# One unread product ahead of every chunk of 24 weight products in the feed-forward up stages

## The chip, the cores and the metric

One core of a Trainium2 chip runs the whole network in one launch. The metric is the device time of a launch in microseconds (us); lower is better.

## What is computed

256 tokens of 1024 features, float32, go through two blocks of two layers each. The feed-forward layers, whose up stages the change touches, are these (cut from the reference):

```python
def conv_ffn(x, w_up, conv_w, conv_b, w_down):            # D_FF = 2816
    h = x @ w_up                                          # 1024 -> 5632
    h = lax.conv_general_dilated(h, ...) + conv_b         # 3 taps along the tokens
    gate, up = jnp.split(h, 2, axis=-1)
    return (jax.nn.silu(gate) * up) @ w_down

def swiglu(n, w_gate, w_up, w_down):
    return (jax.nn.silu(n @ w_gate) * (n @ w_up)) @ w_down
```

The first block has two layers, each a mixer (a gated recurrence, then a sparse attention) followed by `conv_ffn`. The second block has two layers of `swiglu`, a mixer (a spatial gating, then an attention over shared keys and values) and `swiglu` again; so there are four `swiglu` layers. Every layer's input is normed by the token's root mean square. Between the third `swiglu` layer's input and the second attention stand the shared keys, computed from the same tokens.

## The kernel before, in words

**Products.** Every weight product is done in two parts: weights and inputs are each split into a float32r part `hi` and a rest `lo`, and `hi*hi + hi*lo + lo*hi` is summed in PSUM. `unit` (L229) fetches 256 columns of a matrix for 1024 rows (1 MB, issued on SyncE's queue), writes `whi` on ScalarE (L249) and `wlo` on VectorE (L251). There are three buffers for fetched weights and four for each split part. `feat` (L255) does one chunk: for 8 blocks of 128 rows the three products L263, L264 and L265, each with 128x128 weights as the loaded operand and 256 tokens as the moving one: 24 products. `feat2` (L267) does the two chunks of a unit into the halves of one PSUM bank. `down` (L545) and `tok` (L280) do the same with the tokens loaded and 256 weight columns moving (L565 to L567, L576 to L578, L289 to L291).

**Up stages.** `conv_ffn` (L663) takes 11 steps `i`; each step has two units, gate and up, each followed by VectorE's and ScalarE's work on the result. `swiglu` (L626) takes 11 steps too, with L655 and L658 scaling the two results by the token factors. In the second, third and fourth `swiglu` layer (`p.halves`) the first step has a form of its own: it goes by token with `tok_turn` (L613), one tile of 128 tokens after the other; ScalarE's L645 and VectorE's L646 make `ffu` for each tile, and four transposes (L650) turn it into features. Behind its two tiles the program writes `p.finish()`, which broadcasts the token factors on TensorE (L370, copied to `rb` by ScalarE at L446) and, in the third `swiglu` layer, turns the input of the shared keys as well (`pre_half`, L407, transposes L412, splits L306 and L308). In that layer the shared keys themselves (`shared_kv`, L1497, with column sums L365, L1506, L1516 and the rotation product L1489) are written ahead of step 3. The first `swiglu` layer follows `block1_end` (L1315): the end of the first block norms the sum and forms one token factor from two (L1337 to L1341), and the broadcast L370 is the last TensorE work that the program writes ahead of the layer's first step. Here the first step has the common form.

**Order.** The program is written in one order; a compiler pass with a model of time then decides the order on every engine, taking an instruction that is ready ahead of one that is not, the earlier written one first. Where the program wants an order on TensorE, it ties what follows to the last TensorE instruction that it has written so far:

```python
    def behind(s):
        pe = mybir.EngineType.PE
        return s.tc.issue_after(next(i for i in reversed(s.nc.cur_bb.bb.instructions) if i.engine == pe))
```

Before the change the common `feat2` of the up stages has no such tie. PSUM has eight banks: four for `acc`, two for `mx` (transposes), two for `pr` (small products, broadcasts).

**The third mixer's bias rows.** Behind the first `conv_ffn` the program writes a table of 3 MB to DRAM (L1056); the sparse attention reads it back, and the queue of SyncE holds weights of that attention behind the reading.

Of the kernel before, what the change touches and what calls it, by code (L numbers as in the profile page):

```python
# [15 lines left out]
P = 128  # L16
D = 1024
T = 256
# [17 lines left out]
# buffers by tag: a tag's tiles are handed out in the order of the program  # L36
# [9 lines left out]
# a step's later parts, in steps behind its first, and the steps before which the queries' products come  # L46
# [7 lines left out]
# V values, N turned latent of the queries, P their rope part, R its rope, Q queries, S scores, T turned, O out  # L54
# [67 lines left out]
class Feat:  # L122
    """1024 or more features by 256 tokens, two chunks of 128 features to a tile"""
# [14 lines left out]
class Split:  # L138
    """a Feat in two parts, hi and lo, whose sum it is"""
# [8 lines left out]
class Net:  # L148
    def __init__(s, tc, ctx, a):
        s.tc, s.nc, s.a = tc, tc.nc, a  # L150
        s.posted = False
# [7 lines left out]
    # ---- tiles  # L159
# [32 lines left out]
    def behind(s):  # L192
        """what follows on TensorE is queued behind the last of its instructions so far"""
        pe = mybir.EngineType.PE
        return s.tc.issue_after(next(i for i in reversed(s.nc.cur_bb.bb.instructions) if i.engine == pe))

    def warm(s, n):
        """n products that nobody reads, behind the last of TensorE's instructions so far: its clock halves at rest"""
        if n:
            with s.behind():  # L200
                ps = s.prod()
                x = s.ident.bitcast(BF16)
                for _ in range(n):
                    s.nc.tensor.matmul(ps[:, :T], x[:, :P], x, start=True, stop=True)

    # ---- weights
    def fetch(s, parts, k0, nk, cuts=1):
        """columns of matrices, side by side, for k of 128 rows: on their way"""
# [14 lines left out]
    def begin(s, p, fine=0):  # L223
        """a layer: the first of its weights are split in smaller pieces"""
# [3 lines left out]
    def unit(s, parts, k0, nk, fetched=None):  # L228
        """the same, split in two"""  # L229
# [13 lines left out]
        with ExitStack() as stack:  # L243
            # behind what the layer waits for
# [10 lines left out]
    def feat(s, w, c, x, ps):  # L255
        """ps[c-th 128 columns of w, tokens] = w^T x over the unit's k."""
# [10 lines left out]
    def feat2(s, w, x, c=0, beside=None):  # L267
        """two chunks of columns in one bank; beside() after each, in this order on TensorE"""
        ps = s.acc()
        s.parts(lambda j: s.feat(w, c + j, x, ps[:, j * T:(j + 1) * T]), beside)  # L270
# [9 lines left out]
    def tok(s, w, cols, t, x, ps, ks=None):  # L280
        """ps[tokens of tile t, cols of w] = x^T w over the unit's k."""
# [11 lines left out]
    def tok2(s, w, x, beside=None):  # L293
        """both tiles of tokens by the 256 columns of a unit, in one bank"""
# [8 lines left out]
    def split_scaled(s, parts):  # L303
        """(hi, lo, source, scale) of several chunks: a tile's parts are all written before they are read"""
# [6 lines left out]
    # ---- norms  # L311
    class Sum:
        """squares summed over chunks; the last chunk is left apart"""

    def sumsq(s, sm, src, k, n, scale=None):
# [3 lines left out]
        if k == n - 4:  # L319
            # the table of the square root, ahead of its use  # L320
# [8 lines left out]
    def rsqrt(s, out, ss, n, eps, factor=1.0):  # L329
        """out = factor * (ss / n + eps) ** -0.5 on small tiles."""  # L330
# [14 lines left out]
    def rsqrt_v(s, out, ss, n, eps):  # L345
        """the same on VectorE alone: a first guess from the bits, then Newton's steps"""
# [13 lines left out]
    def colsum(s, sm, st):  # L360
        """per-token sums of feature-major tiles -> [128 tokens, 2] in a bank"""
# [5 lines left out]
    def bcast(s, r, st):  # L367
        """[128 tokens, 2] -> [128, 256] of a bank, the same on all partitions"""
# [12 lines left out]
    class Pre:  # L381
        """the input of a layer, normed and split: x(k). The token's factor is left to its consumer:
        r by token, rb along the free axis"""
# [8 lines left out]
    def pre_group(s, p, n, sums=True, bank=None):  # L392
        """256 features of h, turned and split, and their squares' sums"""
# [13 lines left out]
    def pre_half(s, p, t, m, sums=True):  # L407
        """the same for a half of the features of a tile of tokens"""
# [15 lines left out]
    def squares(s, ss, src, n):  # L424
        """the sums of squares by token of a group of 256 features, src by token tile"""
# [3 lines left out]
        if n == 2:  # L429
            # the table of the square root, ahead of its use  # L430
# [20 lines left out]
    # ---- start  # L451
    def load_vectors(s, g, parts, queue):
        """rows of 128 values -> one column of s.vectors each"""
# [81 lines left out]
    def conv_vectors(s, l):  # L535
        """the taps and biases of a layer's convolution"""
# [7 lines left out]
    # ---- feed-forward layers  # L544
    def down(s, w, hid, kn, out, n_beside=0):  # L545
        """out(n, ps) for the 4 groups of 256 columns of hid @ w, hid of kn chunks; ps by token tile"""
# [4 lines left out]
        for n in range(4 - out.late):  # L551
            both = n < n_beside
            if both:
                # the two tiles in one bank, zeroed for both: a chunk of hid serves both at once
# [25 lines left out]
        # the last units: a tile of tokens to its end, then the other  # L580
# [32 lines left out]
    def tok_turn(s, p, units, t, ps, at=()):  # L613
        """both units side by side for a tile of tokens, what p has left to do before the k's in at"""
# [11 lines left out]
    def swiglu(s, p, wg, wu, wd, out, beside=None):  # L626
# [3 lines left out]
        for i in range(KF // 2):  # L630
# [4 lines left out]
            if p.halves and i == 0:  # L635
                # by token: the first tile of tokens is there before the second
# [17 lines left out]
            ps = s.feat2(s.unit([(wg, i * T, T)], 0, KD), p.x)  # L654
            nc.vector.tensor_tensor(h2(g), h2(ps), s.rb2(p), op=OP.mult)  # L655
            nc.scalar.activation(g, g, AF.Silu)
            ps = s.feat2(s.unit([(wu, i * T, T)], 0, KD), p.x)
# [5 lines left out]
    def conv_ffn(s, p, l, out):  # L663
# [12 lines left out]
        for i in range(KF // 2):  # L676
            if l == 0 and i in (3, 6):
                # those of the next one
# [7 lines left out]
            for y, first in zip(ys, (0, KF)):  # L686
                c = first + 2 * i
                ps = s.feat2(s.unit([(w, c * P, T)], 0, KD), p.x)
# [25 lines left out]
    # ---- first block, layer 0  # L714
    def hgrn(s, p, first):
# [40 lines left out]
        def decay(pr):  # L756
            """the logarithms, summed from the start of a chunk"""
# [11 lines left out]
            # exp(x - bk) = k exp(x - b)  # L769
# [4 lines left out]
        def query(pr):  # L774
            """without the tokens' factor"""
# [5 lines left out]
        def offsets():  # L781
            """what lies between a chunk of 32 and the border of the two tiles of 128 tokens"""
# [990 lines left out]
```

## Time and profile before

| | |
|---|---|
| median of 2 runs | 1663.08 us (1660.65 and 1665.51) |
| profiled execution | span 1657.0 us, first to last instruction; its own time beside the span is not listed |
| TensorE busy | 1619.9 us, 98% of the span |
| VectorE busy | 1150.6 us, 69% |
| ScalarE busy | 913.8 us, 55% |
| mean granted TensorE clock | 0.994 |

The timed runs are whole launches and so longer than the span of the profile. In the profile PE is TensorE's products, PEld its weight loads, DVE VectorE, ACT ScalarE. Products overlap in the pipeline, and each is shown with 0.28 us though the next one starts long before its end; so prices are read from start to start. A plain f32 product shows as two records, a float32r or bf16 product and a transpose as one.

### The profile page before, as it was taken

How to read it: one execution, taken by the hardware profiler on the slowest of the kernel's cores; microseconds unless marked ns; L12 is line 12 of the kernel's file. 1: busy time of each engine (PE TensorE's matmuls, PEld its weight loads, DVE VectorE, ACT ScalarE, POOL GpSimd, SP SyncE). 2: the span in 40 equal slices, each digit the busy share in tenths (PEclk: the TensorE clock that was granted, in tenths of full speed). 3: DMA queues.
4: the chain of work that ended last, by engine and by line, in shares of the span. 5: the costliest groups of instructions: out<-in, count | busy, mean ns of one | idle time of the engine just before them, and what ended most of it. 6: DMA issues, size and time to landing. Idle time of an engine off the chain costs nothing.

```text
span 1657.0 us, 34152 instructions
## 1 busy us (share of the span) xinstructions
PE 1619.9 (98%) x14500; PEld 1606.8 (97%) x14502; DVE 1150.6 (69%) x1900; ACT 913.8 (55%) x1443; POOL 6.7 (0%) x28
## 2 busy tenths in 40 slices
PE   8989999995999999999999999999999999999998
PEld 7989999995999999999999999999999999999998
DVE  6986899654859886766667857664686647677653
ACT  7865766453656656544465546444564446665442
POOL 0000000000000000000000000000000000000000
PEclk9999999997999999999999999999999999999999
DMA  8731755678446566566847565556376565447562
GB/s 266 217 100 53 228 188 187 191 154 190 136 136 218 174 202 192 184 192 193 250 144 228 178 191 172 185 171 203 124 241 188 195 201 142 154 133 227 184 202 71
DMA packets 303821, 297.58 MB, mean 180 GB/s; under 512 B 14295, under 2 KB 300214, under 8 KB 303670
## 3 DMA queue, kind: packets, MB, share of 16 engines
q1 hardware_dynamic: 303622, 295.40, 57.8%
q8 instruction: 114, 1.87, 0.5%
q14 instruction: 37, 0.30, 0.1%
q10 hardware_dynamic: 48, 0.01, 0.0%
HBM read 291.19 MB, written 4.19 MB: 178 GB/s over the span
## 4 chain that ended last, share of the span: by engine, by line
PE 91%; DVE 3%; DMA 3%; ACT 2%; issue 1%; SPq 0%; DVEq 0%; ACTq 0%
PE acc L265 16%; PE acc L263 16%; PE acc L264 16%; PE acc L565 8%; PE acc L567 7%; PE acc L566 7%; PE acc L289 3%; PE acc L290 3%; PE acc L291 3%; DMA bias_rows<-rrow 2%; PE acc L576 2%; PE acc L578 2%; PE acc L577 1%; DVE wlo L251 1%; ACT whi L249 1%; PE pr L844 1%
## 5 line engine op out<-in xcount | busy, mean ns | idle before, releaser
L249 ACT ACTIVATE whi<-wst 128x2048 fp32r<-128x2048 f32 (+4 forms) x404 | 524.2, 1331 | 507.1 <-issue 225.3
L251 DVE TENSOR_TENSOR wlo<-wst,whi 128x2048 fp32r<-128x2048 f32 (+4 forms) x404 | 620.9, 1560 | 247.4 <-ACT whi L249 245.6
L263 PE MATMUL acc<-xh,whi 128*128 128x256 f32 x2416 | 671.9, 279 | 1.3 <-ACT xh L306 0.9
L264 PE MATMUL acc<-xl,whi 128*128 128x256 f32 x2416 | 671.8, 279 | 1.0 <-DVE xl L308 1.0
L265 PE MATMUL acc<-xh,wlo 128*128 128x256 f32 x2416 | 671.3, 279 | 0.5 <-DVE wlo L251 0.5
L264 PEld LDWEIGHTS acc<-xl,whi 128*128 128x128 f32 x2416 | 456.1, 189 | 1.7 <-DVE xl L308 1.4
L263 PEld LDWEIGHTS acc<-xh,whi 128*128 128x128 f32 x2416 | 453.4, 188 | 2.0 <-ACT xh L306 1.1
L265 PEld LDWEIGHTS acc<-xh,wlo 128*128 128x128 f32 x2416 | 454.2, 188 | 0.9 <-DVE wlo L251 0.7
L567 PE MATMUL acc<-wlo,fh 128*128 128x256 f32 x880 | 245.0, 279 | 0.0
L566 PE MATMUL acc<-whi,fl 128*128 128x256 f32 x880 | 244.1, 278 | 0.0
L565 PE MATMUL acc<-whi,fh 128*128 128x256 f32 x880 | 244.0, 278 | 0.0
L567 PEld LDWEIGHTS acc<-wlo,fh 128*128 128x128 f32 x880 | 165.2, 188 | 0.0
L566 PEld LDWEIGHTS acc<-whi,fl 128*128 128x128 f32 x880 | 165.1, 188 | 0.0
L565 PEld LDWEIGHTS acc<-whi,fh 128*128 128x128 f32 x880 | 164.9, 188 | 0.0
L289 PE MATMUL acc<-whi,xh 128*128 128x256 f32 x384 | 108.9, 283 | 0.0
L290 PE MATMUL acc<-whi,xl 128*128 128x256 f32 x384 | 107.0, 279 | 0.0
L291 PE MATMUL acc<-wlo,xh 128*128 128x256 f32 x384 | 107.0, 279 | 0.0
L289 PEld LDWEIGHTS acc<-whi,xh 128*128 128x128 f32 x384 | 72.1, 188 | 0.2
L290 PEld LDWEIGHTS acc<-whi,xl 128*128 128x128 f32 x384 | 72.1, 188 | 0.0
L291 PEld LDWEIGHTS acc<-wlo,xh 128*128 128x128 f32 x384 | 72.1, 188 | 0.0
L658 DVE TENSOR_TENSOR ffu<-acc,rb 128x512 f32<-128x512 f32 x41 | 28.3, 690 | 46.5 <-PE acc L265 46.4
L308 DVE SCALAR_TENSOR_TENSOR xl<-mx,vectors,xh 128x128 fp32r<-128x128 f32 (+1 forms) x124 | 39.1, 375 | 22.9 <-ACT xh L306 22.8
(422 smaller groups left out, 2116.6 us busy)
## 6 DMA issues: line engine op xcount, KB each, us to landing
wst<-in_ffn_w_up_dram SPq DMA_DIRECT2D x88, 1024.0 KB, 5.3
wst<-in_ffn_w_down_dram SPq DMA_DIRECT2D x48, 1024.0 KB, 5.4
wst<-in_ffn_w_gate_dram SPq DMA_DIRECT2D x44, 1024.0 KB, 5.4
wst<-in_ffn_w_down_dram SPq DMA_DIRECT2D x24, 768.0 KB, 4.8
wst<-in_gmlp_w_in_dram SPq DMA_DIRECT2D x16, 1024.0 KB, 5.6
wst<-in_hgrn_w_in_dram SPq DMA_DIRECT2D x13, 1024.0 KB, 5.7
wst<-in_gmlp_w_out_dram SPq DMA_DIRECT2D x8, 1024.0 KB
wst<-in_dsa_w_in_dram SPq DMA_DIRECT2D x6, 1024.0 KB
```

What stands on the lines that cost most here:

```text
L249: s.nc.scalar.activation(hi[:, c], w[:, c], AF.Copy)
L251: s.nc.vector.tensor_tensor(lo[:, c], w[:, c], hi[:, c].bitcast(F32), op=OP.subtract)
L263: mm(ps, wh[:, k, cols], xh, start=k == 0, stop=False)
L264: mm(ps, wh[:, k, cols], xl, start=False, stop=False)
L265: mm(ps, wl[:, k, cols], xh, start=False, stop=k == nk - 1)
L289: mm(ps, xh[:, ts], wk, start=k == 0, stop=False)
L290: mm(ps, xl[:, ts], wk, start=False, stop=False)
L291: mm(ps, xh[:, ts], lk, start=False, stop=k == nk - 1)
L308: b = s.nc.vector.scalar_tensor_tensor(lo, src, g, hi.bitcast(F32), op0=OP.mult, op1=OP.subtract)
L565: mm(ps[t], xh, wh[:, k], start=k0 + k == 0 and not both, stop=False)
L566: mm(ps[t], xl, wh[:, k], start=False, stop=False)
L567: mm(ps[t], xh, wl[:, k], start=False, stop=k0 + k == kn - 1 and (t == 1 or not both))
```

## The change

`Net.between` (new) puts one product into a `pr` bank that nobody reads, tied behind the last TensorE instruction written; its kind goes round seven: none; bf16 with 64 columns; bf16 with 32 loaded and 32 moving columns; float32r with 16, 64 and 192 columns; bf16 with 128. All but the third load 128 columns. `feat2` gets an argument with which it calls `between` ahead of each of its two chunks and ties the chunk behind it. The calls in both up stages ask for it, `conv_ffn` from its second step on, `swiglu` in all steps of the common form. Comments are taken out elsewhere, which is not shown.

```diff
-        s.posted = False
+        s.posted, s.shape = False, 0
...
+    def between(s, x):
+
+        n, s.shape = s.shape, (s.shape + 1) % 7
+        mm = s.nc.tensor.matmul
+        with s.behind():
+            if n == 0:
+                return
+            ps = s.prod()
+            xh = x(0)[0]
+            if n == 1:
+                mm(ps[:, :64], s.identb, s.identb[:, :64], start=True, stop=True)
+            elif n == 2:
+                mm(ps[:32, :32], s.identb[:, :32], s.identb[:, :32], start=True, stop=True)
+            elif n == 3:
+                mm(ps[:, :16], xh[:, :P], xh[:, :16], start=True, stop=True)
+            elif n == 4:
+                mm(ps[:, :64], xh[:, :P], xh[:, :64], start=True, stop=True)
+            elif n == 5:
+                mm(ps[:, :192], xh[:, :P], xh[:, :192], start=True, stop=True)
+            else:
+                mm(ps[:, :P], s.identb, s.identb, start=True, stop=True)
+
+    def feat2(s, w, x, c=0, beside=None, between=False):
+
         ps = s.acc()
+        if between:
+            for j in range(2):
+                s.between(x)
+                with s.behind():
+                    s.feat(w, c + j, x, ps[:, j * T:(j + 1) * T])
+            return ps
         s.parts(lambda j: s.feat(w, c + j, x, ps[:, j * T:(j + 1) * T]), beside)
         return ps
...
-            ps = s.feat2(s.unit([(wg, i * T, T)], 0, KD), p.x)
+            ps = s.feat2(s.unit([(wg, i * T, T)], 0, KD), p.x, between=True)
...
-            ps = s.feat2(s.unit([(wu, i * T, T)], 0, KD), p.x)
+            ps = s.feat2(s.unit([(wu, i * T, T)], 0, KD), p.x, between=True)
...
-                ps = s.feat2(s.unit([(w, c * P, T)], 0, KD), p.x)
+                ps = s.feat2(s.unit([(w, c * P, T)], 0, KD), p.x, between=i > 0)
```

## Rows read from the trace of the kernel before

**Rows 1.** The page: span, busy time by engine, and the chain by engine.

```profile
PE 1619.9 (98%) x14500; PEld 1606.8 (97%) x14502; DVE 1150.6 (69%) x1900; ACT 913.8 (55%) x1443; POOL 6.7 (0%) x28
...
PE 91%; DVE 3%; DMA 3%; ACT 2%; issue 1%; SPq 0%; DVEq 0%; ACTq 0%
```

**Rows 2.** Timeline of TensorE, 250 to 256 us: start, duration, what.

```profile
249.73 0.28 PE L265 MATMUL acc<-xh,wlo 128*128 128x256 f32 x1
...
255.96 0.28 PE L263 MATMUL acc<-xh,whi 128*128 128x256 f32 x1
```

**Rows 3.** The page's groups: VectorE's scaling of the gated layers' up products.

```profile
L658 DVE TENSOR_TENSOR ffu<-acc,rb 128x512 f32<-128x512 f32 x41 | 28.3, 690 | 46.5 <-PE acc L265 46.4
```

**Rows 4.** Timeline of TensorE, 1233 to 1235 us.

```profile
1233.31 0.28 PE L365 MATMUL pr<-col,sqa 128*128 128x1 f32 x2
...
1234.44 0.28 PE L263 MATMUL acc<-xh,whi 128*128 128x256 f32 x1
```

**Rows 5.** The chain in order of time: start, duration, what.

```profile
90.45 1.48 PE pr L844 x64
```

**Rows 6.** Timeline of TensorE, 447 to 449 and 1416 to 1418 us.

```profile
448.36 0.39 PE L556 MATMUL acc<-cst,zero 128*128 128x512 bf16 x1
...
448.71 0.28 PE L566 MATMUL acc<-whi,zl 128*128 128x256 f32 x1
...
1416.35 1.03 PE L1489 MATMUL mx<-qrx,cst 128*128 128x256 f32 x4
1417.22 0.27 PE L1629 MATMUL acc<-maskb,identb 128*128 128x256 bf16 x1
```

**Rows 7.** Timelines of TensorE and VectorE, 665 to 679 us, first gated layer.

```profile
666.09 0.28 PE L263 MATMUL acc<-xh,whi 128*128 128x256 f32 x1
...
677.84 0.61 PE L370 MATMUL pr<-cst,f 128*128 128x128 f32 x4
678.21 0.37 PE L263 MATMUL acc<-xh,whi 128*128 128x256 f32 x1
...
674.66 0.16 DVE L1341 TENSOR_TENSOR f<-f,rc 128x2 f32<-128x2 f32 x1
```

**Rows 8.** Timelines of TensorE and VectorE, second and fourth gated layer.

```profile
1010.25 0.37 PE L263 MATMUL acc<-xh,whi 128*128 128x256 f32 x1
...
1018.28 0.38 PE L650 MATMUL mx<-cst,ffu 128*128 128x128 f32 x2
...
1016.49 0.48 DVE L646 SCALAR_TENSOR_TENSOR ffu<-acc,pr,ffg 128x256 f32<-128x256 f32 x1
...
1480.67 0.36 PE L263 MATMUL acc<-xh,whi 128*128 128x256 f32 x1
...
1486.64 0.48 DVE L646 SCALAR_TENSOR_TENSOR ffu<-acc,pr,ffg 128x256 f32<-128x256 f32 x1
```

**Rows 9.** Timelines of TensorE and VectorE, third gated layer, second step.

```profile
1199.83 0.37 PE L263 MATMUL acc<-xh,whi 128*128 128x256 f32 x1
...
1210.64 0.60 PE L650 MATMUL mx<-cst,ffu 128*128 128x128 f32 x4
...
1206.56 2.15 DVE L308 SCALAR_TENSOR_TENSOR xl<-mx,vectors,xh 128x128 fp32r<-128x128 f32 x8
```

**Rows 10.** Timelines of VectorE and TensorE, shared keys; in brackets idle time before it.

```profile
1228.97 0.69 DVE L1506 TENSOR_TENSOR kc<-acc,rb 128x512 f32<-128x512 f32 x1 [0.66 <-PE acc L265]
...
1233.07 0.42 DVE L1516 TENSOR_TENSOR krx<-acc,rb 128x256 f32<-128x256 f32 x1
...
1235.82 0.59 PE L1489 MATMUL mx<-krx,cst 128*128 128x256 f32 x2
```

**Rows 11.** Windows: stretch, its us, busy us of PE, PEld, DVE, ACT, POOL, granted clock, DMA.

```profile
380.00:382.00 2.00, 0.00 (x0) 0.00 (x0) 0.00 (x0) 0.00 (x0) 0.00 (x0) 0.53 0.88 101
395.00:397.00 2.00, 2.00 (x11) 2.00 (x11) 1.82 (x5) 0.00 (x0) 0.00 (x0) 0.50 1.08 346
```

**Rows 12.** Who waited for whom on TensorE: us in total, times, longest.

```profile
PE pr L1106 <- ACT drl L1109: 17.0, 2, 16.0
```

More of the change, by code (lines that the diff above doesn't have):

```diff
@@ L265, in feat @@
             mm(ps, wl[:, k, cols], xh, start=False, stop=k == nk - 1)
-    def feat2(s, w, x, c=0, beside=None):
-        ps = s.acc()
+    def between(s, x):
[19 more added lines that the diff above has]
+    def feat2(s, w, x, c=0, beside=None, between=False):
+        ps = s.acc()
+        if between:
[4 more added lines that the diff above has]
+            return ps
         s.parts(lambda j: s.feat(w, c + j, x, ps[:, j * T:(j + 1) * T]), beside)
@@ L312 @@
     class Sum:
+        pass
     def sumsq(s, sm, src, k, n, scale=None):
@@ L381 @@
     class Pre:
+        pass
     def pre(s, gain):
```

## The prediction

> **What bounds the kernel now.** I read the page's busy table and its chain first. TensorE is busy for 98% of the span and holds 91% of the chain that ended last [rows 1]. So whatever takes TensorE's time, or makes it stand, goes to the end nearly in full; what VectorE or ScalarE gain or lose counts only where TensorE waits for them. Next comes the price of a product. In an up stage the timeline has one start after the other: 56 products of 256 columns start between 249.73 and 255.96 us, which is 6.23 / 55 = 0.113 us each [rows 2]. A chunk of 24 is 2.72 us. Last I read the few places where TensorE's order in the trace differs from the order in which the program writes its products, because the change ties that order down [rows 7 to 10].
>
> **The change, part one: the products.** The two layers with a convolution call the new form in 10 of 11 steps, twice a step, two chunks a call: 80 chunks. The four gated layers call it in every step that runs the L655/L658 path; L658 ran 41 times [rows 3], so 41 x 2 x 2 = 164 chunks. Of 244 chunks every seventh, from the first on, gets nothing (35), so 209 products are added: 35 of each kind from one to five and 34 of the sixth.
>
> What a narrow product costs beside weight products is to be read where one already stands between them. In the shared-key part eight records with one moving column and 128x128 weights (L365) and two weight products start between 1233.31 and 1234.44 us: ten in 1.13 us, 0.113 us each [rows 4]. One column costs as much as 256. The stream goes at the pace of the weight loads, and each new product brings one, whatever it moves. A bf16 product of 512 columns between weight products (L556) shifts what follows: from its start to that of L566 there is 0.35 us, which holds it and one weight product, so 0.35 - 0.113 = 0.24 us [rows 6]. That is its columns, with hardly anything for the change of type. So I take 0.113 us for the five kinds of up to 128 columns: 174 x 0.113 = 19.7 us.
>
> The kind with 192 float32r columns is the open one, for the trace has no float32r product under 256 columns. If it goes as those of 256 do, it is 0.113 us. Plain f32 goes slower: four records of 256 columns (L1489, two per product) take 1416.35 to 1417.22, 0.2175 us each [rows 6]; by that pace 192 columns are 0.163 us a record, 0.33 us with two. I take one record at that pace, 0.16 us, between the two: 35 x 0.16 = 5.6 us. Part one is 25.3 us. The ends: if a narrow product needs no load period of its own it might cost as little as the 32-column products of L844, 64 in 1.48 us or 0.023 us [rows 5], 4.8 us for all 209; if float32r under 256 columns is always two plain records, the 70 of the third and fourth kind gain 0.113 us each and the 35 of the fifth 0.166 us, and the part is 39 us. The row with 128-column loads (L365) is the nearest, so I stay with 25.3. Nothing hides it: all of it stands on the engine that sets the end.
>
> The Trainium skill has a rule that would make it cheaper: "TensorE: Matmul & The Clock Gate", section "Back-to-back issue gap", gives isolated gaps of about 60 cycles for up to 64 columns and 134 for 128. By it, as an estimate from that page, 140 x 0.025 + 35 x 0.083 + 34 x 0.056 = 8.3 us. The row of L365 disagrees with it (0.113 us for one column), and the same section says that the isolated gap counts too little where every product has its own load.
>
> **Part two: the order.** Each new product, and each chunk behind it, is queued behind the last TensorE instruction that the program has written so far. Inside a stage this changes nothing, since chunks run in program order already. It does where the program writes, ahead of a chunk, TensorE work that has to wait, and where the compiler until now pulled chunks in front of it. There are five such places.
>
> (a) Start of the first gated layer of the second block. Its first step has the new form too, and the last TensorE work written ahead of it is the broadcast of the token factors (L370). Before, the step's 96 products start at 666.09 and the broadcast comes behind them, at 677.84 [rows 7]. The factor is ready when L341's chain ends with L1341, 674.66 + 0.16 = 674.82. Now the products wait for that and four records: 675.35. With 96 x 0.118 = 11.3 us (their pace from 666.09 to 677.84, four transposes among them) they end at 686.65 where before all was past at 678.21: 8.4 us.
>
> (b, c) Second step of the second and of the fourth gated layer. The first step goes by token, and its hidden part is turned (L650) behind VectorE's L646. Before, the second step starts at 1010.25 and the second pair of turns comes at 1018.28, in its midst [rows 8]. L646 ends at 1016.49 + 0.48 = 1016.97, late because weight splits are queued ahead of it on ScalarE and VectorE; these wait for no product of the second step, so the delay stays. The turns can start at about 1017.1 and the step at 1017.3: 7.0 us later, less 0.22 us for the pair that moved, 6.8. In the fourth layer it is 1486.64 + 0.48, and 0.3 more, 1487.4 for 1480.67 [rows 8]: 6.6 us.
>
> (d) Second step of the third gated layer. The same turns stand behind the transposes for the shared keys, whose two banks are freed by VectorE's L308; eight of these end at 1206.56 + 2.15 = 1208.71. The step can start at 1209.3 where it started at 1199.83 [rows 9]. Of the 9.5 us, 12 records (1.4 us) are work that moved ahead of it: 8.1 us.
>
> (e) Fourth step of that layer, behind the rotation of the shared keys (L1489). VectorE's L1506 shows the last chunk ahead done at 1228.9, the next ends 2.7 us later, at 1231.6, and L1489 waits for L1516 until 1233.49 [rows 10]; start at 1233.95, less 1.3 us for L365 and L1489, which fill the gap: 1.0 us.
>
> Together 30.9 us. In (a) to (d) TensorE rests for some 6 us and more. After its long rest in the third mixer the granted clock, which is 1.00 (2.4 GHz) in work, was 0.53 in 380 to 382, and back at work it was still 0.50 (1.2 GHz) in 395 to 397, with 11 records in these 2 us, where the full clock runs 17 [rows 11]. About 1.5 us of products are lost at such a return; 4 x 1.5 = 6.0 us (ends: none, and 8 if the slow stretch lasts longer). The ends of part two are 20 us (splits ordered anew, so that L646 comes some us sooner) and 45 us (the compiler, with TensorE standing, fills ScalarE and VectorE with still more splits ahead of what it waits for). The weights in turn arrive earlier than needed and no other wait goes.
>
> **Sum.** 25.3 + 30.9 + 6.0 = 62.2 us. The profiled execution has a span of 1657.0 us; its own time beside the span isn't given, and the two timed runs, 1660.65 and 1665.51, lie 3.6 and 8.5 us above it. The difference goes on their median: 1663.1 + 62.2 = 1725.3 us, 3.7%. A measurement of this kernel can tell about 2%, 33 us, from no change.
>
> **Rivals.** *Two records (0.13).* Narrow float32r products go as plain f32 in two records: 39 us for part one, 1739 us. For it: f32 products do show as two records; against it: the weight products don't. *In the shadow (0.08).* Short products slip in at L844's pace, 4.8 us, and only the order costs: 1663.1 + 4.8 + 36.9 = 1705 us. For it: nothing but those rows, whose loads have 32 columns; L365 speaks against it. By the gap rule of the Trainium skill the end would be near, at 1708 us. *Order as before (0.06): not slower by what can be told.* The one mechanism is the place where the five waits end. If the compiler, finding TensorE idle, puts the gate's activation and L646 ahead of the weight splits, and brings the chain of (a) forward likewise, the turns come as soon as the token products end; or the ties bind nothing at run time. Then only the products count, 1663.1 + 25.3 = 1688 us, 1.5%. It decides once the waits and slow returns fall from 37 to under 8 us (33.3 - 25.3). For it: TensorE's order is planned, and a new plan may differ. Against it: in both layers [rows 8] L646 comes 6 us behind the step's start, behind splits that no part of the change touches. *The long wait shifts (0.04).* TensorE waits 16.0 us in the third mixer for L1109 [rows 12], which stands behind weights queued behind the bias rows. A changed model time might order those two transfers otherwise, and the wait would go with its slow return: 17.5 us less, 1708 us. Against: the distance between that transfer and the layer around it isn't touched.
>
> **How the numbers follow.** The forecast has 0.69, with 1710 to 1742 as its own range from the ends of part two and of the 192-column kind. The whole range reaches down past the shadow and the shifted wait and up past two records: 1701 to 1747; the case of 1688 and the far end of both upper bounds are left out. Within 2% lies only the fourth case and a sliver of the shadow: 0.07. Faster by over 2% needs a gain that I can't name: 0.01. Slower by over 2%: 0.92.
>
> **What would show it.** Right: the chunks' first products start about 0.113 us later behind kinds one to four and six; L370 stands in front of the first product of the gated layers' first stage; L650 stands in front of each second step; gaps of 6 to 8 us on TensorE with a clock of 0.5 behind them; PE's busy share falls by some two points. Wrong: second steps that still start ahead of the last L650, gaps under 3 us, narrow products at 0.03 us or at 0.23, a kind of 192 columns at 0.33, or a new wait in the middle of a stage.

## The result: 1737.7 us, slower by 4.5%, and the profile after

The changed kernel takes 1737.74 us (two runs, 1737.33 and 1738.16) where the kernel before took 1663.08: ratio 1.0452, 95% interval 1.0402 to 1.0503. The profiled span went from 1657.0 to 1736.4 us, +79.4. The forecast was 1725.3 us with 1710 to 1742 as its own range. Lines of the new kernel stand 28 below those of before from `feat2` on (L370 is L398, L650 is L678); the six kinds of new product are L277, L279, L281, L283, L285 and L287.

The page of the kernel after, busy time by engine and the chain that ended last (of before: [rows 1]):

```profile
PE 1669.2 (96%) x14709; PEld 1645.4 (95%) x14711; DVE 1154.8 (67%) x1900; ACT 911.8 (53%) x1443; POOL 6.7 (0%) x28
...
PE 71%; ACT 3%; DVE 1%; issue 1%; DVEq 0%
```

TensorE has the 209 records more that were counted, 49.3 us more busy time, and two points less of the span: it also stands still for longer. Who it waits for is in the waits of TensorE after: us in total, times, longest.

```profile
PE mx L678 <- DVE ffu L674: 13.0, 2, 6.5
PE pr L398 <- DVE f L1369: 7.5, 1, 7.5
PE mx L440 <- DVE xl L336: 6.8, 1, 6.8
...
PE acc L264 <- DVE xl L336: 2.4, 5, 0.6
...
PE acc L263 <- ACT xh L334: 1.1, 2, 0.8
PE mx L1517 <- DVE krx L1544: 1.0, 1, 1.0
```

The first three and the last are the five places of the prediction (the 13.0 us are two, (b) and (c)), 28.3 us together. Of the 2.4 and 1.1 us for xl and xh, 2.4 stand at the start of the two convolution layers' up stages, where before TensorE had no rest: places that the prediction doesn't have. The same in TensorE's timeline, with the idle time before an instruction in brackets:

```profile
688.87 1.22 PE L398 MATMUL pr<-cst,f 128*128 128x128 f32 x4 [7.49 <-DVE f L1369]
...
689.74 0.36 PE L281 MATMUL pr<-xh 128*128 128x16 f32 x1
...
1048.77 0.69 PE L678 MATMUL mx<-cst,ffu 128*128 128x128 f32 x2 [6.50 <-DVE ffu L674]
...
1250.00 1.12 PE L440 MATMUL mx<-cst,h 128*128 128x128 f32 x4 [6.84 <-DVE xl L336]
```

In [rows 7] the stage's products came first and the broadcast L370 behind them; now L398 stands in front of the first of them, and TensorE rests 7.5 us ahead of it. In [rows 8] the second step was under way when the turns L650 came; now L678 comes first. Behind these rests the granted clock is low. Windows of the kernel after, the columns as in [rows 11]:

```profile
688.90:692.60 3.70, 3.70 (x18) 3.70 (x19) 0.00 (x0) 0.38 (x1) 0.00 (x0) 0.51 0.00 0
...
1048.80:1054.20 5.40, 5.40 (x26) 5.40 (x27) 2.89 (x2) 2.31 (x2) 0.00 (x0) 0.50 1.05 329
1054.20:1058.00 3.80, 3.80 (x33) 3.75 (x33) 0.38 (x1) 0.49 (x1) 0.00 (x0) 0.99 0.85 274
1250.00:1255.70 5.70, 5.70 (x26) 5.38 (x27) 4.90 (x10) 2.65 (x6) 0.00 (x0) 0.50 0.91 205
...
1550.30:1556.50 6.20, 6.20 (x29) 5.93 (x30) 2.89 (x2) 2.40 (x2) 0.00 (x0) 0.53 1.00 301
```

PE is busy all the time in the four stretches at half speed, with half the records. Length times what the clock lacks: 1.8 + 2.7 + 2.85 + 2.9 = 10.3 us, where the prediction had 6.0.

What a product costs is read from start to start. Two weight products take two starts' distance, 0.227 us; with one new product between them the timeline of the kernel after has, for the kind with 32 loaded columns and for the one with 16 float32r columns:

```profile
1103.67 0.28 PE L265 MATMUL acc<-xh,wlo 128*128 128x256 f32 x1
1103.88 0.19 PE L279 MATMUL pr<-identb 128*32 128x32 bf16 x1
1104.00 0.39 PE L263 MATMUL acc<-xh,whi 128*128 128x256 f32 x1
1104.22 0.28 PE L264 MATMUL acc<-xl,whi 128*128 128x256 f32 x1
...
1106.72 0.28 PE L265 MATMUL acc<-xh,wlo 128*128 128x256 f32 x1
1106.84 0.17 PE L281 MATMUL pr<-xh 128*128 128x16 f32 x1
1106.87 0.36 PE L263 MATMUL acc<-xh,whi 128*128 128x256 f32 x1
1107.07 0.28 PE L264 MATMUL acc<-xl,whi 128*128 128x256 f32 x1
```

1104.22 - 1103.67 = 0.55, so 0.32 us for the first; 1107.07 - 1106.72 = 0.35, so 0.12 us for the second. The starts behind a product take some steps to become even, so the price of a kind is taken from the weight product ahead to the fourth behind, less four steps of 0.1133 us (to the second behind it comes out up to 0.02 us lower). Over all that stand among weight products (33 to 35 of each kind) the medians are 0.147 us for kind one, 0.327 for kind two, 0.127 for three, 0.137 for four, 0.127 for five (192 columns) and 0.137 for six: 35 x 0.865 + 34 x 0.137 = 34.9 us, where the prediction had 25.3.

Where the 79.4 us lie, from the first and last weight product of each stage (us against the kernel before; the experiments' columns are for the next section):

| stage | after | ties alone | products alone | one product per start |
|---|---|---|---|---|
| up, first convolution layer | +10.0 | +6.9 | +6.9 | +0.5 |
| its down stage | 0.0 | +0.1 | +0.7 | -0.1 |
| up, second convolution layer | +4.4 | +1.2 | +2.8 | -3.6 |
| its down stage | -0.6 | 0.0 | -0.6 | -0.8 |
| up, first gated layer | +17.7 | +15.1 | +6.9 | +0.3 |
| its down stage | 0.0 | +2.2 | 0.0 | 0.0 |
| down stage of the spatial gating | 0.0 | -0.1 | 0.0 | -1.5 |
| up, second gated layer | +12.8 | +4.7 | +2.8 | -3.6 |
| its down stage | -2.2 | -2.3 | 0.0 | -2.2 |
| up, third gated layer | +18.4 | +12.6 | +6.3 | +0.2 |
| its down stage | +2.2 | 0.0 | +2.2 | +0.1 |
| up, fourth gated layer | +16.4 | +7.8 | +6.6 | +0.3 |

Down stages that the change doesn't touch became shorter or longer by more than 2 us: something that the prediction had no term for.

### The profile page after: what moved, and what is told of

The parts are those of the page before. It is cut to its first block, busy times and chain, and to the rows that moved or that the text cites. A ratio compares the mean times of both kernels' runs of the same rounds, so it can differ in the third digit from the quotient of the medians.

```text
span 1736.4 us, 34568 instructions
## 1 busy us (share of the span) xinstructions
PE 1669.2 (96%) x14709; PEld 1645.4 (95%) x14711; DVE 1154.8 (67%) x1900; ACT 911.8 (53%) x1443; POOL 6.7 (0%) x28
## 4 chain that ended last, share of the span: by engine, by line
PE 71%; ACT 3%; DVE 1%; issue 1%; DVEq 0%
PE acc L263 14%; PE acc L264 13%; PE acc L265 13%; PE acc L593 6%; PE acc L594 6%; PE acc L595 6%; ACT whi L249 2%; PE acc L604 1%; PE acc L606 1%; PE acc L605 1%; PE acc L319 1%; PE acc L317 1%; PE acc L318 1%; PE acc L1199 1%; DVE wlo L251 1%; PE mx L1227 1%
## 5 line engine op out<-in xcount | busy, mean ns | idle before, releaser
L263 PE MATMUL acc<-xh,whi 128*128 128x256 f32 x2416 | 695.2, 288 | 1.4 <-ACT xh L334 1.1
L264 PEld LDWEIGHTS acc<-xl,whi 128*128 128x128 f32 x2416 | 461.9, 191 | 3.6 <-DVE xl L336 3.4
L263 PEld LDWEIGHTS acc<-xh,whi 128*128 128x128 f32 x2416 | 459.0, 190 | 3.4 <-ACT xh L334 1.5
L683 DVE TENSOR_TENSOR ffg<-acc,rb 128x512 f32<-128x512 f32 x41 | 28.4, 692 | 61.3 <-PE acc L265 34.3
```

Of the source, the lines that this page charges most:

```text
L263: mm(ps, wh[:, k, cols], xh, start=k == 0, stop=False)
L264: mm(ps, wh[:, k, cols], xl, start=False, stop=False)
```

## The experiments

The theory at this point: the time is the sum of the products' price, the waits of the ties and the half clock behind them. The rivals: the products or the ties alone explain nearly all.

**Ties alone.** No product; the ties as in the change.

```diff
-        n, s.shape = s.shape, (s.shape + 1) % 7
+        n, s.shape = 0, (s.shape + 1) % 7
```

> The ties of the change without any of its products. Theory of the ties: the five waits come as in the changed kernel (7.5, 6.5, 6.5, 6.8 and 1.0 us, 28 in all), with the half clock behind four of them (some 10 us) and 2 to 3 us at the start of the first convolution layer, so about 40 us more than before, 1700 to 1706 us; the up stages between go at the paces of before. Rival, the products disturb: the waits are the products' doing, and ties alone stay within 8 us of before.

Measured: 1708.78 us (ratio 1.025, 1.0216 to 1.0285), span 1706.1, +49.1 us. The five waits are there, 6.2 to 7.5 us for the four long ones, with the half clock behind them; the products aren't needed for that. The time lies above the expected 1706 us, and that the up stages keep their paces didn't hold: from start to start the weight products of the first convolution and of the first gated layer came 0.1178 us apart where before it was 0.1133, and those of the second gated layer the other way. With the down stages that changed likewise this makes some 4.6 us. Behind the wait (e) the clock was at half for 3.4 us too, which in the changed kernel it was not.

**Products alone.** The new form from the third step on, and not in the third gated layer's fourth: 181 products remain, at places where the order before was already that of the program.

```diff
-... p.x, between=True)
+... p.x, between=i > 1 and not (beside and i == 3))
...
-                ps = s.feat2(s.unit([(w, c * P, T)], 0, KD), p.x, between=i > 0)
+                ps = s.feat2(s.unit([(w, c * P, T)], 0, KD), p.x, between=i > 1)
```

> The products where nothing written ahead of them has to wait: from the third step of every layer on, and not in the fourth step of the third gated layer: 212 chunks, some 182 products. Theory of the ties: no wait on TensorE above 1 us that before had not; 182 products at 0.163 us in the mean are 30 us, and the two paces (0.113 and 0.118 us a product) even out to within 5 us: 1688 to 1699 us. Rival, the products disturb: over 1715 us. Priced by the prediction's 0.12 us a product: 1685 us.

Measured: 1694.19 us (1.0171, 1.0148 to 1.0195), span 1692.3, +35.3. All five waits are gone and the mean clock is back at 0.994. 30 or 31 of each kind at their prices are 30.2 us; some 5 us are something else, 2.2 of them in the third gated layer's down stage, where no product was added. So neither rival holds: the ties alone make 49.1 us and the products alone 35.3.

**Without the 32-column kind.** As the change, but the kind n = 2 is left out as n = 0 is.

```diff
-            if n == 0:
+            if n in (0, 2):
                 return
```

> The changed kernel without its 35 products of 32 loaded columns. If each costs 0.33 us, as its starts in the trace say (the load of 32 columns isn't taken ahead of the product before it), 11.4 us go: about 1726 us. If it costs what the prediction took, 0.113 us, 4 us go: 1734 us. The pace behind it (0.113 us) stays as it was, since it was 0.113 ahead of it too.

Measured: 1724.78 us (1.0356, 1.0335 to 1.0376), span 1724.0, 12.4 us under the span of the change. 35 x 0.327 = 11.4: a sixth of the products made a third of part one.

**Each kind three times in a row.** The starts in an up stage come either 0.1133 us apart or 0.1178, for hundreds of products in a row at the full clock. In the changed kernel the pace behind a kind is the same every time: 0.1178 behind kinds three and six and in the chunk without a product, which comes behind six, and 0.1133 behind the other four. Here the products alone are used, in another order, to tell whether a product flips the pace or sets it.

```diff
-        n, s.shape = s.shape, (s.shape + 1) % 7
+        order = (1, 1, 1, 3, 3, 3, 4, 4, 4, 5, 5, 5, 6, 6, 6, 2, 2, 2, 0)
+        n, s.shape = order[s.shape], (s.shape + 1) % 19
```

> The same places as the kernel with products only, but each kind three times in a row (bf16 64, float32r 16, 64, 192, bf16 128, then 32 loaded columns, then one chunk with none). It asks what a product does to the pace of the chunk behind it, 0.113 or 0.118 us a product. Theory of the switch: the kinds that changed the pace (bf16 64 and 128, float32r 16 and 64) turn it over each time, so that three in a row alternate; those with 192 and with 32 loaded columns leave it or set it. Theory of the setting: each kind sets one pace whatever was ahead (bf16 64 and float32r 64 the fast one, float32r 16 and bf16 128 the slow one), so that the chunks behind three in a row are alike. Rival, the pace belongs to the stage (its weights and transfers): it doesn't follow the kinds. Prices as in the changed kernel, 0.12 to 0.14 us, and 0.33 for 32 loaded columns; about 1663 + 212 x 0.154 = 1696 us.

Measured: 1691.17 us (one run), span 1689.4. TensorE's timeline, for three products of 16 float32r columns in a row: each with the fourth and the 22nd weight product behind it.

```profile
1067.29 0.17 PE L282 MATMUL pr<-xh 128*128 128x16 f32 x1
...
1067.75 0.28 PE L263 MATMUL acc<-xh,whi 128*128 128x256 f32 x1
...
1069.87 0.28 PE L263 MATMUL acc<-xh,whi 128*128 128x256 f32 x1
...
1070.23 0.17 PE L282 MATMUL pr<-xh 128*128 128x16 f32 x1
...
1070.70 0.28 PE L263 MATMUL acc<-xh,whi 128*128 128x256 f32 x1
...
1072.74 0.28 PE L263 MATMUL acc<-xh,whi 128*128 128x256 f32 x1
```

18 paces take 2.12 us behind the first (0.1178 each) and 2.04 behind the second (0.1133); behind the third it is 0.1178 again. The kind of 16 columns turns the pace over, all 33 times. The others don't: behind bf16 of 64 columns, float32r of 64 and 192 and the 32-column kind it was 0.1133 every time, behind bf16 of 128 columns 0.1178 every time, whatever the pace ahead (float32r of 192 columns always had 0.1133 ahead, so for it that isn't shown). So neither "flips" nor "sets" holds for all kinds. The same two paces are in the kernel before. Its windows over 20 us of the first gated layer's down stage and of the second's up stage:

```profile
820.00:840.00 20.00, 20.00 (x179) 20.00 (x178) 8.52 (x10) 8.70 (x14) 0.00 (x0) 1.00 0.70 211
...
1040.00:1060.00 20.00, 20.00 (x172) 20.00 (x172) 13.37 (x11) 8.41 (x8) 0.00 (x0) 1.00 0.59 192
```

The clock is 1.00 and PE is full in both, yet one has 179 records and the other 172. Before, the up stages of the first convolution layer and of the first, third and fourth gated layer ran at 0.1133, those of the second convolution and the second gated layer at 0.1178.

**One product of 64 float32r columns at stage starts**, on the kernel before and without ties, into the bank whose first product overwrites it: in 12 places of the up stages, two in each, and in 16 of the down stages.

```diff
+    def pace(s, ps, x):
+        xh = x(0)[0]
+        s.nc.tensor.matmul(ps[:, :64], xh[:, :P], xh[:, :64], start=True, stop=True)
...
         ps = s.acc()
+        if pace:
+            s.pace(ps, x)
...
                 ps = [s.acc()[:, :T], s.acc()[:, :T]]
+                if n == 0 or not out.late:
+                    s.pace(ps[0], hid)
```

> The kernel before with 25 or so unread float32r products of 64 columns and no ties, at the start of up and down stages, each into the bank that the next product overwrites. The traces show the 256-column products of a stage coming either every 0.1133 us or every 0.1178 us for hundreds in a row, and in the trace with each kind three times running a float32r product of 64 columns was followed by 0.1133 each time, from either pace. Theory (the product sets the pace): about 3,500 products of the kernel before that ran at 0.1178 behind these places (the up stage of the second convolution layer, two thirds of both its down stages, the first feed-forward layer's second mixer, the gated layer's down stage) come 0.0045 us sooner, 15.7 us, less 25 x 0.135 = 3.4 us for the products: 1651 us beside a kernel before at 1663, and the trace shows 0.1133 through those stages. Rival A (every added product flips the pace): stages that were fast become slow, some 3,000 products lose what others gain, 1661 to 1675 us. Rival B (the pace hangs on something else, and the products only cost their time): 1666 us.

**The same with bf16 and 128 columns.**

```diff
-        s.nc.tensor.matmul(ps[:, :64], xh[:, :P], xh[:, :64], start=True, stop=True)
+        s.nc.tensor.matmul(ps[:, :P], s.identb, s.identb, start=True, stop=True)
```

> The same places as in the run with 64 float32r columns, but the product is the bf16 one of 128 columns, behind which the traces show 0.1178 us each time, from either pace. Theory (the product sets the pace): some 5,300 products that ran at 0.1133 behind these places go to 0.1178, 24 us, and 25 x 0.13 us for the products: 1688 to 1692 us beside a kernel before at 1663. Rival A (every added product flips the pace): as the run with 64 columns, 1661 to 1675 us. Rival B (only their time): 1666 us.

Measured: 1662.74 us with 64 columns (1.0026, 1.001 to 1.0042) and 1676.4 with 128 (1.011, 1.0085 to 1.0135). Neither is the theory's number; the first lies in the range of the rival by which every product turns the pace over. But the 13.7 us between two kernels that differ in the shape of 28 products are more than the products cost. The traces say where the theory fails. With 64 columns all 12 up stages' places are followed by 0.1133, as expected, nine of them from 0.1133, which refutes that rival for this kind, and the up stages of the second convolution and the second gated layer are 3.6 us shorter each; but the down stages, where the tokens are loaded and weights move, go on at 0.1178 behind it, so the gated layers' down stages are 2.3 us longer each where they had been at 0.1133. With 128 columns 9 of the 12 places are followed by 0.1178 and 3 by 0.1133. What a product does to the pace hangs on what stands around it too.

**Which loads are dear.** The products alone, with seven other kinds.

```diff
+            if n == 0:
+                mm(ps[:, :32], s.identb, s.identb[:, :32], start=True, stop=True)
+            elif n == 1:
+                mm(ps[:32, :P], s.identb[:, :32], s.identb, start=True, stop=True)
+            elif n == 2:
+                mm(ps[:32, :32], s.identb[:, :32], s.identb[:, :32], start=True, stop=True)
+            elif n == 3:
+                mm(ps[:64, :64], s.identb[:, :64], s.identb[:, :64], start=True, stop=True)
+            elif n == 4:
+                mm(ps[:96, :P], s.identb[:, :96], s.identb, start=True, stop=True)
+            elif n == 5:
+                mm(ps[:32, :64], xh[:, :32], xh[:, :64], start=True, stop=True)
+            else:
+                mm(ps[:, :T], xh[:, :P], xh, start=True, stop=True)
```

> As the run with the products alone, clear of the waits, but with seven other kinds in turn, in order: bf16 128 columns loaded and 32 moved; 32 loaded and 128 moved; 32 and 32; 64 and 64; 96 loaded and 128 moved; float32r 32 loaded and 64 moved; float32r 128 loaded and 256 moved. It tells what made the 32-column product cost 0.327 us where the others cost 0.12 to 0.147. Theory (a load of fewer than 128 columns is not pulled ahead of the product before it, and neither is the load behind it): 32/128, 32/32, 64/64, 96/128 and float32r 32/64 cost 0.3 to 0.4 us each, 128/32 costs 0.12 to 0.15, and 128/256 costs 0.113 to 0.118. Rival (the few columns moved leave no time for the load behind it): 128/32 costs 0.3 us too, and 32/128 and 96/128 cost 0.12 to 0.15.

Measured: 1703.69 us (one run), span 1701.9. The timeline for three of the kinds, each between the weight product ahead of it and the second behind it:

```profile
1108.20 0.28 PE L265 MATMUL acc<-xh,wlo 128*128 128x256 f32 x1
1108.40 0.22 PE L281 MATMUL pr<-identb 128*64 128x64 bf16 x1
...
1108.77 0.28 PE L264 MATMUL acc<-xl,whi 128*128 128x256 f32 x1
...
1111.27 0.28 PE L265 MATMUL acc<-xh,wlo 128*128 128x256 f32 x1
1111.38 0.22 PE L283 MATMUL pr<-identb 128*96 128x128 bf16 x1
...
1111.61 0.28 PE L264 MATMUL acc<-xl,whi 128*128 128x256 f32 x1
...
1114.20 0.28 PE L265 MATMUL acc<-xh,wlo 128*128 128x256 f32 x1
1114.32 0.19 PE L285 MATMUL pr<-xh 128*32 128x64 f32 x1
...
1114.54 0.28 PE L264 MATMUL acc<-xl,whi 128*128 128x256 f32 x1
```

0.57, 0.34 and 0.34 us, so 0.34, 0.11 and 0.11 for the product. The medians, taken to the fourth weight product behind as above: bf16 with 32 loaded columns 0.367 (128 moved) and 0.327 (32 moved), bf16 with 64 loaded 0.347; but bf16 with 96 loaded 0.127, float32r with 32 loaded 0.127, bf16 with 128 loaded and 32 moved 0.137, float32r of full size 0.137. Both readings fall: few moved columns cost nothing extra, and neither do all loads under 128 columns. Dear are the bf16 loads of 32 and 64 columns. The weight loads (PEld) of the same three places show how, each with the next weight load behind it:

```profile
1108.40 0.11 PEld L281 LDWEIGHTS <-identb 128*64 128x64 bf16 x1
1108.55 0.19 PEld L263 LDWEIGHTS acc<-xh,whi 128*128 128x128 f32 x1
...
1111.27 0.12 PEld L283 LDWEIGHTS <-identb 128*96 128x96 bf16 x1
1111.38 0.19 PEld L263 LDWEIGHTS acc<-xh,whi 128*128 128x128 f32 x1
...
1114.20 0.11 PEld L285 LDWEIGHTS pr<-xh 128*32 128x32 f32 x1
1114.32 0.19 PEld L263 LDWEIGHTS acc<-xh,whi 128*128 128x128 f32 x1
```

The two cheap loads start together with the product ahead of them (1111.27, 1114.20), and the load behind them starts together with their own product (1111.38, 1114.32). The dear load starts only 0.20 us behind the product ahead (1108.40 for 1108.20), and the load behind it 0.15 us behind its own product (1108.55 for 1108.40): both loads stand in the stream instead of beside it. In the median of each dear kind it is 0.20 us for the first, and 0.12 to 0.16 for the second. Why these loads and not float32r of 32 columns wasn't found.

**One product per start, in up stages alone.** The kernel with 64 columns without its products at the down stages, and one of bf16 with 128 columns at the spatial gating's down stage, which that kind had left at 0.1133.

```diff
-                if n == 0 or not out.late:
-                    s.pace(ps[0], hid)
+                if n == 0 and kn == 16:
+                    mm(ps[0][:, :P], s.identb, s.identb, start=True, stop=True)
```

> The kernel before with the unread float32r product of 64 columns at the starts of up stages alone (12 places), and one bf16 product of 128 columns at the start of the gated layer's down stage, where the run with 128 columns had left the stage at 0.1133 us; none at the other down stages, where the run with 64 columns left 0.1178 us behind every one of them. From the stages of those two traces against the kernel before: second convolution layer -3.6 and -0.6 us, the second mixer of the first feed-forward layer -3.5 and -2.3, the gated layer's down stage -1.5, the other up stages +0.3 to +0.6 each, sum -10 us: a span near 1647 and 1648 to 1653 us, 0.5 to 0.8% below the kernel before, with the runs closer together than those of the kernel before, since what decides the pace of a stage is now in the program. Rival (a pace is not handed from an up stage to the down stage behind it, or a down stage's pace hangs on something else): the down stages stay at 0.1178, 1655 to 1660 us.

Measured: 1648.11 us (11 runs, 1647.49 to 1649.57) beside 1659.45 for the kernel before (22 runs, 1652.33 to 1668.43): 0.993, 0.9908 to 0.9951, span 1645.8. The same 20 us of the second gated layer's up stage:

```profile
1040.00:1060.00 20.00, 20.00 (x179) 20.00 (x178) 13.13 (x11) 7.85 (x8) 0.00 (x0) 1.00 0.58 186
```

Stage by stage (last column of the table) it is as expected. All 11 runs lie under the fastest of the 22 before. 13 products that nobody reads make the kernel 0.7% faster than before.

**Filling two of the waits.** The ties alone, and 50 products that nobody reads in front of the turns for which (b) waits, and 50 at (c).

```diff
                 p.finish()
+                s.warm(0 if beside else 50)
                 for t in range(2):
```

> The run with the ties alone, with 50 products that nobody reads put in front of the four transposes for which the queue waits 6.2 us at the second mixer of both feed-forward layers. They take about 5.6 us, in time in which TensorE did nothing. Theory (the wait costs its own length and then the half clock behind it): the granted clock stays at full speed behind these two waits, 2.5 and 2.9 us come back, and the rest of the time stays: about 1703.5 us beside 1708.8 with the ties alone (ratio to the kernel before 1.022 where that had 1.025), and no stretch at 0.50 behind these two places. Rival A (the half clock is not what the idle time does, or costs nothing): same as the ties alone, 1707 to 1710. Rival B (the fill delays what the queue waits for): over 1712.

Measured: 1700.54 us (4 runs, 1694.99 to 1709.01), ratio 1.0259, 1.0217 to 1.0301, where the ties alone had 1.025: from the times alone it can't be told, since other stages took other paces. The windows can. Ties alone, then filled, right behind the wait (b):

```profile
1043.00:1046.00 3.00, 2.93 (x14) 2.93 (x15) 1.02 (x2) 2.40 (x2) 0.00 (x0) 0.50 1.09 350
```

```profile
1043.00:1046.00 3.00, 2.52 (x22) 2.52 (x23) 1.04 (x3) 2.40 (x2) 0.00 (x0) 1.00 1.09 350
```

The clock stays at 1.00, and the second gated layer's up stage is 1.9 us shorter than with the ties alone, the fourth's 1.5 us, both at 0.1133 in both kernels. The expected 5.4 us were taken from the changed kernel; with the ties alone the stretches at half clock were shorter (some 4.3 and 3.7 us, so 2.1 and 1.8 us lost), and the turns came 0.3 us later behind the fill. Of the half clock's price nearly all came back, and the wait stayed.

**Ties at the convolution layers' second step alone**, the place that the prediction left out.

```diff
-... p.x, between=True)
+... p.x)
...
-                ps = s.feat2(s.unit([(w, c * P, T)], 0, KD), p.x, between=i > 0)
+                ps = s.feat2(s.unit([(w, c * P, T)], 0, KD), p.x, between=i == 1)
```

> Ties alone, and only at the second step of the two convolution layers (16 of the 212 chunks), the place that the prediction did not count. Theory (the place costs what its waits show): the trace has the waits on xl and xh at the start of both layers again, up to 0.8 us each, the up stage of the first layer 2 to 3 us longer and that of the second about 1.2 us, apart from 0.0045 us for every 256-column product whose pace has changed: 1666 to 1672 us beside 1663. Rival (these waits only take the place of idle time that was there before): no stage longer once the paces are put right, 1661 to 1665.

Measured: 1667.34 us (1.0056, 1.0031 to 1.008). Its timeline has the waits again, of which the first three cost 1.8 us in a row:

```profile
173.82 0.38 PE L264 MATMUL acc<-xl,whi 128*128 128x256 f32 x1 [0.44 <-DVE xl L336]
...
176.07 0.50 PE L263 MATMUL acc<-xh,whi 128*128 128x256 f32 x2 [0.82 <-ACT xh L334]
...
177.08 0.38 PE L264 MATMUL acc<-xl,whi 128*128 128x256 f32 x1 [0.51 <-DVE xl L336]
```

The first layer's up stage is 6.8 us longer, but about 980 of its products went from 0.1133 to 0.1178, 4.4 us; 2.4 remain. The second's is 1.35 us longer at the same pace: 3.7 us for the place. The same trace shows how free the pace is: the fourth gated layer, with the same order as before, ran at 0.1178 here and was 3.5 us longer in its up stage and 2.3 us in its down stage.

## Why the prediction was right, and where its terms were off

The account of the 79.4 us of span: products 34.9, the five waits 28.3, the half clock 10.3, the convolution layers' starts 3.7, the paces 2.1; sum 79.3. That it comes out to 0.1 us is luck (some 1 us of the prices of kinds three and six is pace as well), but the same terms give 10.0, 4.6, 17.6, 12.4, 18.3 and 17.0 us for the six up stages, where the table has 10.0, 4.4, 17.7, 12.8, 18.4 and 16.4. The paces are worked out so: of seven chunks three (behind kinds three and six and behind none) ran at 0.1178. In the four stages that had been at 0.1133, 164 chunks, that costs 164 x 3/7 x 24 x 0.0045 = 7.6 us; in the two that had been at 0.1178 the other four of seven gain 80 x 4/7 x 0.108 = 4.9; three down stages add 2.2 - 2.2 - 0.6.

The forecast's terms are 62.2 us, 17.2 short, yet its time is only 12.4 us short. The rest is luck: wherever a run's time and span are both recorded the time is 1.8 us above the span, so the profiled execution of before, with 1657.0, was some 4 us faster than the median that the terms were added to. The range follows from the ends that it names only roughly: they give some 1713 to 1745 us.

**The bound.** That what TensorE gets or waits for goes to the end in full held: the span grew by its 49.3 us of work and 30.1 us of rest, and no transfer is among the new waits.

**Part one, 25.3 us, measured 34.9.** The method was right for loads of 128 columns: 0.127 to 0.147 where the row of L365 [rows 4] gave 0.113, hardly depending on the columns moved. The failed step is "So I take 0.113 us for the five kinds of up to 128 columns": the 32-column kind was put among them though its load is the one that isn't of 128 columns, and it took 0.327 us, 7.5 us more in all. The row of L844 [rows 5], whose loads are of 32 columns, pointed to a lower price if anything, because there such loads follow one another; between loads of 128 columns they are dear. The 192-column kind was put at 0.16 us and took 0.127.

**Part two, 30.9 us, measured 28.3.** (a) 8.4 against 7.5, (b) 6.8 and (c) 6.6 against 6.5 each, (d) 8.1 against 6.8, (e) 1.0 against 1.0. Reading where the trace's order differs from the program's, and asking what the tied work waits for, gave each place and size. But the list wasn't complete ("There are five such places"): the tie at the convolution layers' second step, 3.7 us, is a sixth.

**The half clock, 6.0 us, measured 10.3.** The mechanism held: filling the waits keeps the clock at 1.00 behind them. The size was off, above the bound of 8: the one return of before that it was taken from was at 0.50 for some 3.5 us, which is 1.75 us lost and not 1.5; those of the changed kernel lasted 3.7 to 6.2 us.

**What wasn't in it.** The two paces of the product stream. [Rows 2] gave 0.113 us, [rows 7] had 0.118 ("their pace from 666.09 to 677.84, four transposes among them"), and the difference was put down to the transposes. In the sum it makes 2 us; in a single stage it makes 5.

**The rivals.** *Two records*, 1739 us, lies nearest to the result, by chance, and is wrong all the same: the float32r kinds of 16, 64 and 192 columns are single records of 0.127 to 0.137 us. *In the shadow* falls with every kind over 0.11 us. So do, as a price here, the isolated gaps that the Trainium skill gives in "TensorE: Matmul & The Clock Gate", section "Back-to-back issue gap"; the section's own caution that they count too little where products each bring a load is borne out. *Order as before* falls by the waits, 28.3 us. *The long wait shifts* falls: 16.6 us at L1134 after, 17.0 before [rows 12].

## What to carry to other kernels

Tying TensorE's order to the program's has its price where the compiler had pulled ready work in front of waiting work: list all places where the trace's order and the program's differ, and add to each wait the stretch at half clock behind it, for which one return is a poor measure: those of these kernels lasted 3.2 to 6.2 us. A small product in a stream of products that each bring a load costs the stream's full step whatever it moves, and about three steps if it is bf16 and loads 32 or 64 columns, so leave such shapes out of a stream of 128-column loads. And when the same code shows two paces at a full clock, count records per 20 us in each stage: a cheap product at the start of a stage may choose the better one, which was worth 0.7% here. Which product does it has to be tried at each place, since the same one left the other pace elsewhere.

## What the runs showed of the hardware that was not expected

- A steady stream of 256-column products with a load each runs at 0.1133 or at 0.1178 us a product, clock 1.00 in both, and keeps its pace over 1,400 products. Small products or transposes between change it; which kind leaves which pace was the same in every round of the changed kernel, but differed between up and down stages. What decides it stays open. A stage that wasn't touched took one pace in the trace of one kernel and the other in another's (5.9 us for the fourth gated layer). It was not tried whether that is all of the kernel before's spread of 16 us over 22 runs; with the product at each up stage's start the runs lie within 2.1 us.
- A bf16 product that loads 32 or 64 columns costs 0.33 to 0.37 us between loads of 128 columns, one that loads 96 or float32r with 32 loaded only 0.13. A dear load starts 0.20 us behind the product ahead of it and holds the next load back until 0.12 to 0.16 us behind its own product; with the cheap kinds the next load starts within 0.01 us of it.
- Float32r with 16, 64 or 192 columns costs no more than bf16: 0.127 to 0.137 us.
